# Stacked queries and keys of a differential attention: placed by DMA through DRAM scratch in place of matmuls with a selection matrix

## The chip, the cores and the metric

The kernel is one program on one NeuronCore of a Trainium2 chip (trn2). The metric is the device time of one execution in microseconds (us), taken as the median of several runs. A profile of one execution gives the start, the end and the inferred releaser of every instruction on the five engines: PE (TensorE, matmuls; PEld is its weight load), DVE (VectorE), ACT (ScalarE), POOL (GpSimd) and SP (SyncE, which here does nothing but issue DMAs).

## The reference, cut to what matters

The network has two layers of width 1024 on 512 latent tokens and 256 context tokens. In each layer one input projection feeds three groups of heads: neighbourhood attention, differential attention and gated linear attention. Only the differential attention is touched. It has four heads, each with two components of 32 features, and subtracts a second softmax from a first one:

```python
def diff_weights(q, k, lam):
    s = jnp.einsum('bhcqd,bhckd->bhcqk', q, k).astype(F32) * (q.shape[-1] ** -0.5)
    p = jax.nn.softmax(s, axis=-1)
    return p[:, :, 0] - lam * p[:, :, 1]
...
    qb = rope_2d(rms_norm(_diff_heads(pl['qb']), lp['qn_b']), row, col)
    kb = rope_2d(rms_norm(_diff_heads(pl['kb']), lp['kn_b']), row, col)
    vb = _heads(pl['vb'], DA_HEADS, DA_V_DIM)
...
    o_b = diff_attention_latent(qb, jnp.concatenate([kb, kb_c], axis=3),
                                jnp.concatenate([vb, vb_c], axis=2), lam)
```

In the first layer the context tokens have queries too (768 query tokens), in the second only the latent ones (512). There are always 768 keys.

## The kernel before

A float32 value goes through the matmuls as two parts, a rounded high part and the low rest, so that a product of two values is the sum of high x high, high x low and low x high. A projection is therefore three matmuls for each block of rows (`gemm_steps`, L251 to L253). For the scores of one component of 32 features the kernel packs the four terms into one matmul with 128 rows: the queries stand as high, low, high, low and the keys as high, low, low, high, 32 rows each. These 128-row operands are called stacks. One preparation (`da_prep`, two heads, letter `d` in the order for the first pair and `D` for the second) makes four components of queries and four of keys; it runs four times, twice in each layer.

In the kernel before a stack is filled by TensorE: for a component and a stretch of 512 or 256 tokens, two matmuls with a 32-row selection matrix `stk` copy the high and low parts `hl` onto the right 32-row blocks of a PSUM tile (L770), and DVE (L772) or ACT (L774) casts that tile into the stack tile `st`.

The mixer of a layer is a weave. TensorE's order is written out by hand as a string, `ORDER`: a count advances the stream of projections by so many steps (three matmuls of 512 columns or six of 256), a letter advances one of the threads by one `yield`. Letters of a thread that has ended do nothing. The threads are `d`/`D` (this preparation), `a`, `b` (scores and softmax of the two differential heads, L800), `n`, `l`, `r` (preparation and two heads of the neighbourhood attention), `g` to `q` (gated linear attention). The projections (`pj` for queries and keys, `pjv` for values) go to DRAM through a single tile `x`, from where the threads fetch them again as `xi`, `xv`, `vt`. Every 12 steps a block of the modulation's weights (`ar`, L274, L276) is multiplied in between.

The order on the other engines and on SP is set by a scheduler from its own estimates. All DMAs stand in SP's one queue, in that order, and SP waits at each for what it needs. Projection weights arrive as `wr` (L239) and are split into `wh` and `wl`; `wr` and `ar` share two buffers. The stack tiles `st` share seven buffers with tiles of the other threads; `hl` shares three buffers under the name `P`.

Of the kernel before, what the change touches and what calls it, by code (L numbers as in the profile page):

```python
# [10 lines left out]
F32 = mybir.dt.float32  # L11
F32R = mybir.dt.float32r
# [19 lines left out]
# row blocks of the output projection: those of the heads that are done first, and the last ones  # L32
OUT_A, OUT_B = (0, 1, 2, 3, 4, 5), (6, 7)
# dot products of the modulation's columns: along with a pair of blocks of the MLP, along with a block of its second product
CUTS = 2
ADA_F, ADA_D = 4, 2
# the order of the projections
JOBS = ("gates vb ka0 va0 qb1 kb1 kc0 vc0 qc0 qa1 ka1 va1 kc1 vc1 qc1 gc0 gc1 gc2 gc3",
        "qb0 kb0 vb qa0 ka0 va0 qb1 kb1 qa1 ka1 va1 gates kc0 vc0 qc0 gc0 gc1 kc1 vc1 qc1 gc2 gc3")
# the order of the first steps: norm, modulation by columns (scale, shift), rows of the products  # L40
# [13 lines left out]
# blocks of 32 columns whose windows of four say which copies a part of a stack goes to: (queries, keys) x (high, low)  # L54
WINDOWS = (1, 0, 1, 0, 1, 1, 0, 0, 1)
STACK = ((5, 3), (0, 1))

# columns of the packed per-layer vectors
# [7 lines left out]
# column blocks of w_in (128 columns each)  # L66
# [4 lines left out]
class Lay:  # L71
    """Per-layer vectors on chip."""


class Rows:
    """Row blocks of a product's weights on two tiles of four."""
# [7 lines left out]
class Net:  # L84
# [53 lines left out]
    def setup(self, up):  # L138
        """Constants, and the first layer's vectors."""
# [14 lines left out]
    def tokens(self, p, up):  # L154
        """Two row blocks of the tokens."""
        x = up.tile([128, 2, TT], F32, name=f"x{p}")
        self.nc.sync.dma_start(out=x[:, :, :TL], in_=self.A["xT"][:, 2 * p:2 * p + 2])
        self.nc.sync.dma_start(out=x[:, :, TL:], in_=self.A["ctxT"][:, 2 * p:2 * p + 2])
        self.xs[2 * p], self.xs[2 * p + 1] = x[:, 0], x[:, 1]

    def silu_cond(self, up):
        """Twice silu of both conditioning vectors; the selector halves."""
# [6 lines left out]
    def late_consts(self, up):  # L169
# [5 lines left out]
        sk = up.tile([128, 288], F32, name="sk")  # L175
        self.nc.sync.dma_start(out=sk, in_=self.A["stk"])
        self.stk = self.cp.tile([128, 288], F32R, name="stk")
        self.V.tensor_copy(self.stk, sk)
# [12 lines left out]
    def layer_consts(self, y, up):  # L191
# [17 lines left out]
        # halved convolution weights (column 3 * f + j) and biases  # L209
# [4 lines left out]
    def newton(self, src, n, d):  # L214
        """rsqrt(src / d + EPS) of a compact [128, n]."""
# [8 lines left out]
        # a step of third order (to 8 / 3 of the root), and one of second order  # L224
# [21 lines left out]
    def gemm_steps(self, ps, w, ah, al):  # L246
        """A product; yields after every few steps of it."""
# [18 lines left out]
    def ada_part(self, y, part, pool, bufs):  # L266
        """A sixth of the modulation, 256 columns on each column tile; yields after every block of rows."""
# [22 lines left out]
    def ada_cols(self, fp, parts):  # L290
        """Sixths of the modulation [(layer, part)], columns on the partitions, by dot products of half columns; yields after each."""
# [24 lines left out]
    def ada_chunk(self, y, part, j, up):  # L316
        """256 columns of a sixth of the modulation: the blocks of rows on four column tiles."""
# [20 lines left out]
    def begin(self, y, up):  # L338
        """The first three products run on the scaled tokens; their outputs take the norm, and the shift's own product."""
# [137 lines left out]
    def seg(self, g):  # L477
        """Stream, first token, operands of a segment."""
        s, t0 = (0, g * TC) if g < 2 else (1, 0)
        sl = slice(t0, t0 + TC)  # L480
        hi, lo = ((self.axh, self.axl), (self.ach, self.acl))[s]
        return s, sl, [t[:, sl] for t in hi], [t[:, sl] for t in lo]

    def norm_bcast(self, accs):
        """PSUM [128, 256]: the reciprocal root mean square of each token on every partition."""
# [12 lines left out]
    def make_xn(self, y, xs, g, which, bc=None):  # L498
        """xs(k): the stream's tile and one for its norm (the same without bc: the tile is normed already)."""
# [30 lines left out]
    def pj(self, y, at, name, block, lat=True, ctx=True, perm=False, scale=1.0):  # L530
        """A block's product, on its way to DRAM, from where the head groups fetch it."""
# [17 lines left out]
    def cuts(self, y, name):  # L549
        """A weight that takes the place of two is made ready in parts."""  # L550
# [4 lines left out]
    def pjg(self, y, at, hd, ctxo):  # L555
        """A head's gate: twice its silu."""
# [14 lines left out]
    def pjv(self, y, at, name, block):  # L571
        """Values of 256 columns, tokens on the partitions."""
# [21 lines left out]
    def gates(self, y):  # L594
        """Low-rank gate activations: the weights' two parts side by side (the next product adds their sums)."""
# [35 lines left out]
    def finish(self, y, at, ctxo):  # L631
        """The heads' outputs as operands of the output projection."""
# [19 lines left out]
    def fetch(self, y, ea, hp, hd, cd):  # L652
        """The residual stream takes the place of the tiles that the heads needed first."""
# [10 lines left out]
    def out_first(self, y, ctxo):  # L664
        """The output projection of the heads that are done first."""
# [7 lines left out]
    def head_rms(self, at, xs, G, d, by=None):  # L673
        """Per (tile, token tile, group): reciprocal root mean squares (of the tile times by), compact. Yields ahead of the product."""
# [40 lines left out]
    def to_tokens(self, out, x, n):  # L715
        """x [128 features, n * 128 tokens] to out [128 tokens, n, 128 features]."""
# [15 lines left out]
    def da_prep(self, y, at, d, pr, ctxq):  # L732
# [8 lines left out]
        # the queries' norms go into the exponentials' scales  # L741
        qn = at.tile([128, TT], F32, tag="xn", name="xn", bufs=self.nxn)[:, :Tq]
        S.activation(qn, xq[:, :Tq], AF.Copy, scale=y.g[:, 1:2])
        for i, Tn in ((0, Tq), (1, TT)):
# [14 lines left out]
            # per component of 32 rows: high | low | high | low against high | low | low | high  # L759
            ss = []  # L760
            for c in range(4):
                rows = slice(32 * c, 32 * c + 32)
                if c % 2 == 0:
                    s = at.tile([128, 2, TT], F32R, tag="st", name="st", bufs=self.nst)
                for t0, n in ((0, TL), (TL, TC))[:1 if Tn == TL else 2]:
                    yield
                    ps = self.pm(n)
                    for a in range(2):
                        w = STACK[i][a] * 32
                        T.matmul(ps, lhsT=self.stk[rows, w:w + 128], rhs=hl[rows, a, t0:t0 + n], start=(a == 0), stop=(a == 1))  # L770
                    if (c + i) % 2:
                        V.tensor_copy(s[:, c % 2, t0:t0 + n], ps)  # L772
                    else:
                        S.copy(s[:, c % 2, t0:t0 + n], ps)  # L774
# [7 lines left out]
        # reciprocals of the first softmaxes' sums  # L782
        d.rs = at.tile([128, 6, 2], F32, tag="rs", name="rs", bufs=2)

    def da_head(self, y, at, d, hh, ctxq):
        V, S, T = self.V, self.S, self.T
        for qt in range((TT if ctxq else TL) // 128):
# [18 lines left out]
            # times the first sum, whose reciprocal the outputs' norms take  # L806
# [13 lines left out]
    def values(self, d, qt, vs, ws):  # L820
        """Both heads' weights times values."""
# [7 lines left out]
    def da_out(self, y, at, d, pr, ctxq):  # L829
        """Norms of the outputs, and of the first softmaxes."""  # L830
# [34 lines left out]
    def na_head(self, y, at, d, pr, hh, ctxq):  # L865
# [3 lines left out]
        for qt in range(Tq // 128):  # L869
# [6 lines left out]
            # the scores' columns: segments (first, count, first key), and those with a bias  # L876
# [49 lines left out]
    def gla_prep(self, y, at, d, pr, ctxo):  # L926
        """Gates: 16 * log decay, then its running sums within chunks of 128, forward and backward."""
# [28 lines left out]
        # decays over whole chunks  # L956
# [5 lines left out]
    def gla_states(self, y, at, d):  # L962
        """States at the chunks' starts, both directions (context chunks are 4 and 5)."""
# [475 lines left out]
```

## Time and profile before

| | us |
|---|---|
| median of 3 runs | 1958.68 |
| lowest and highest run | 1957.72, 1968.63 |
| span of the profiled execution (first to last instruction) | 1956.1 |
| median minus that span | 2.6 |
| PE busy | 1874.8 (96% of the span) |
| DVE busy | 1234.8 (63%) |
| ACT busy | 774.1 (40%) |
| DMA | 217.93 MB, 33.8% of the 16 engines' span |

The runs are a list without a note which of them was profiled, so the profiled execution's own time is read as its span with the 2.6 us that lie between it and the median. Two runs lie within 1 us of each other and the third 10 us above. Busy shares are averages over stages; what a change in one stage is worth is read in that stage, from what its engines wait for.

### The profile page before, as it was taken

To read this page: it belongs to the slowest core of one execution; us is meant where nothing else is said; L and a number is where in the kernel's file an instruction comes from. 1 tells how busy PE (TensorE), PEld (TensorE's weight loads), DVE (VectorE), ACT (ScalarE), POOL (GpSimd) and SP (SyncE) were. 2 spreads that over 40 slices of the span, in tenths; PEclk is the share of its full clock that TensorE was granted. 3 is DMA by queue.
4 is the path that set the end of the run, shared out by engine and by line. 5 is a ranking of instruction groups with operands and counts; after the bars stand their busy time and mean duration, and the time that the engine had idled before them with its cause. 6 is when DMAs were issued, how large, how long until landed. Compare 5 with 4: busy or idle time off the path is not lost. (4 is left out here: it accounts for less than half of the span.)

```text
span 1956.1 us, 33522 instructions
## 1 busy us (share of the span) xinstructions
PE 1874.8 (96%) x13598; PEld 1567.2 (80%) x13598; DVE 1234.8 (63%) x2554; ACT 774.1 (40%) x1350; POOL 107.1 (5%) x134
## 2 busy tenths in 40 slices
PE   8999999896999999999999999999996999999999
PEld 6778878774788888888888987878885788888887
DVE  6437575767669786588577563656576675445353
ACT  4536565455234331232133343645545343223232
POOL 2100000101020000000000110000012020000000
PEclk9989999897999999999999999999998989999999
DMA  9423242326122444234434223222433223332322
GB/s 323 138 92 111 92 146 98 115 98 204 54 74 92 124 129 149 94 125 130 139 109 127 95 68 130 84 81 68 143 106 101 65 72 97 97 97 86 109 94 100
DMA packets 90874, 217.93 MB, mean 111 GB/s; under 512 B 10464, under 2 KB 21472, under 8 KB 90592
## 3 DMA queue, kind: packets, MB, share of 16 engines
q1 hardware_dynamic: 90720, 215.79, 33.8%
q8 instruction: 107, 1.75, 0.4%
q14 instruction: 47, 0.39, 0.1%
HBM read 190.06 MB, written 25.69 MB: 110 GB/s over the span
## 5 line engine op out<-in xcount | busy, mean ns | idle before, releaser
L262 ACT CAST wh<-wr 128x1024 fp32r<-128x1024 f32 (+3 forms) x205 | 200.0, 978 | 415.9 <-PE pg L252 222.2
L263 DVE TENSOR_TENSOR wl<-wr,wh 128x1024 fp32r<-128x1024 f32 (+3 forms) x205 | 232.3, 1137 | 168.4 <-ACT wh L262 166.3
L252 PE MATMUL pz<-axl,wh 128*128 128x512 f32 (+1 forms) x752 | 288.3, 383 | 2.6 <-DVE axl L511 2.5
L251 PE MATMUL pz<-axh,wh 128*128 128x512 f32 (+1 forms) x752 | 287.8, 383 | 0.8 <-ACT axh L510 0.7
L253 PE MATMUL pz<-axh,wl 128*128 128x512 f32 (+1 forms) x752 | 287.0, 382 | 0.0
L252 PEld LDWEIGHTS pz<-axl,wh 128*128 128x128 f32 x752 | 142.3, 189 | 29.6 <-DVE axl L511 4.5
L251 PEld LDWEIGHTS pz<-axh,wh 128*128 128x128 f32 x752 | 142.3, 189 | 27.6 <-ACT axh L510 1.8
L253 PEld LDWEIGHTS pz<-axh,wl 128*128 128x128 f32 x752 | 142.3, 189 | 26.9
L308 DVE SCALAR_TENSOR_TENSOR wj<-wc,cb 128x512 bf16<-128x512 f32 x224 | 154.4, 689 | 6.2 <-DMA wc<-in_w_ada_t_dram 1.0
L251 PE MATMUL pg<-axh,wh 128*128 128x512 f32 x344 | 152.9, 445 | 2.7 <-ACT axh L262 2.5
L252 PE MATMUL pg<-axl,wh 128*128 128x512 f32 x344 | 139.3, 405 | 1.8 <-DVE axl L263 1.8
L253 PE MATMUL pg<-axh,wl 128*128 128x512 f32 x344 | 139.0, 404 | 0.0
L251 PE MATMUL pg<-gh,wh 128*128 128x512 f32 (+1 forms) x352 | 133.3, 380 | 0.0
L253 PE MATMUL pg<-gh,wl 128*128 128x512 f32 (+1 forms) x352 | 132.6, 377 | 0.0
L252 PE MATMUL pg<-gl,wh 128*128 128x512 f32 (+1 forms) x352 | 132.0, 375 | 0.0
L1161 DVE SCALAR_TENSOR_TENSOR h<-pg,ada,h 128x512 f32<-128x512 f32 (+1 forms) x80 | 53.5, 669 | 95.0 <-PE pg L253 94.8
L252 PE MATMUL pm<-acl,wh 128*128 128x256 f32 x352 | 99.8, 283 | 0.0
L253 PE MATMUL pm<-ach,wl 128*128 128x256 f32 x352 | 99.6, 283 | 0.0
L251 PE MATMUL pm<-ach,wh 128*128 128x256 f32 x352 | 99.5, 283 | 0.0
L801 DVE TENSOR_REDUCE sm<-pz 128x1 f32<-128x768 f32 (+1 forms) x80 | 67.4, 847 | 45.2 <-PE pz L800 44.5
L251 PEld LDWEIGHTS pg<-axh,wh 128*128 128x128 f32 x344 | 67.2, 195 | 30.8 <-issue 15.7
L1240 ACT ACTIVATE th<-cv 128x512 f32<-128x512 f32 x66 | 37.0, 561 | 121.2 <-DVE cv L1237 121.2
(387 smaller groups left out, 4194.9 us busy)
## 6 DMA issues: line engine op xcount, KB each, us to landing
wc<-in_w_ada_t_dram SPq DMA_DIRECT2D x112, 256.0 KB, 2.9
wr<-in_w_in_dram SPq DMA_DIRECT2D x45, 512.0 KB, 3.8
wr<-in_w_g_dram SPq DMA_DIRECT2D x44, 512.0 KB, 3.5
wr<-in_w_u_dram SPq DMA_DIRECT2D x44, 512.0 KB, 3.4
wr<-in_w_d_dram SPq DMA_DIRECT2D x31, 448.0 KB, 3.2
ar<-in_w_ada_dram SPq DMA_DIRECT2D x48, 256.0 KB, 3.3
ar<-in_w_ada_dram SPq DMA_DIRECT2D x16, 512.0 KB, 7.5
wr<-in_w_d_dram SPq DMA_DIRECT2D x16, 512.0 KB, 3.5
```

The lines of the kernel that those rows point to most:

```text
L251: self.T.matmul(ps, lhsT=wh[:, k, :], rhs=ah[k], start=(k == 0), stop=False)
L252: self.T.matmul(ps, lhsT=wh[:, k, :], rhs=al[k], start=False, stop=False)
L253: self.T.matmul(ps, lhsT=wl[:, k, :], rhs=ah[k], start=False, stop=(k == n - 1))
L262: self.S.copy(hi, x)
L263: (eng or self.V).tensor_tensor(out=lo, in0=x, in1=hi.bitcast(F32), op=ALU.subtract)
L308: V.scalar_tensor_tensor(out=junk, in0=w, scalar=0.5, in1=cb[:, i, h * 512:h * 512 + 512], op0=ALU.mult, op1=ALU.mult, accum_out=acc[:, k, ...
L801: V.tensor_reduce(out=sm[:, c:c + 1], in_=s, op=ALU.max, axis=AX.X, negate=True)
L1161: self.late = V.scalar_tensor_tensor(out=h, in0=ps, scalar=y.ada[part][:, o, s:s + 1], in1=h, op0=ALU.mult, op1=ALU.add).ins
L1240: S.activation(th, c, AF.Tanh)
```

## The change

The selection matrix, its matmuls and the casts of the stacks go. The high and low parts `hl` are written to a DRAM tile `parts` (high, low, and for the keys high once more), and each half of 64 rows of a stack is read back by one DMA whose source is two consecutive parts of 32 rows each: high and low for the queries' halves and the keys' first half, low and high for the keys' second half. The `yield`s between the old matmuls go with them.

```diff
             hl = at.tile([128, 2, TT], F32R, tag="P", name="hl", bufs=3)
             self.split(xn, hl[:, 0, :Tn], hl[:, 1, :Tn])
-            # per component of 32 rows: high | low | high | low against high | low | low | high
+
+            parts = self.dp.tile([2 + i, 128, TT], F32, name=f"hl{y.l}_{pr}_{i}")
+            nc.sync.dma_start(out=parts.rearrange("a p t -> p a t")[:, :2, :Tn], in_=hl[:, :, :Tn].bitcast(F32))
+            if i:
+                nc.sync.dma_start(out=parts[2, :, :Tn], in_=hl[:, 0, :Tn].bitcast(F32))
             ss = []
             for c in range(4):
-                rows = slice(32 * c, 32 * c + 32)
                 if c % 2 == 0:
                     s = at.tile([128, 2, TT], F32R, tag="st", name="st", bufs=self.nst)
-                for t0, n in ((0, TL), (TL, TC))[:1 if Tn == TL else 2]:
-                    yield
-                    ps = self.pm(n)
-                    for a in range(2):
-                        w = STACK[i][a] * 32
-                        T.matmul(ps, lhsT=self.stk[rows, w:w + 128], rhs=hl[rows, a, t0:t0 + n], start=(a == 0), stop=(a == 1))
-                    if (c + i) % 2:
-                        V.tensor_copy(s[:, c % 2, t0:t0 + n], ps)
-                    else:
-                        S.copy(s[:, c % 2, t0:t0 + n], ps)
+                own = parts[:, 32 * c:32 * c + 32, :Tn]
+                for half, src in ((0, own[:2]), (64, own[i:i + 2])):
+                    nc.sync.dma_start(out=s[half:half + 64, c % 2, :Tn].bitcast(F32), in_=src)
                 ss.append(s[:, c % 2])
             stacks.append(ss)
```

The rest of the diff removes `WINDOWS`, `STACK`, the load of `stk` (one DMA and one cast at the start) and comments. Line numbers of the changed kernel differ: L770 has no successor, the writes are L754 and L756, the reads L763, the scores L789.

What the change does to the order is seen at three places. The first is SP's queue in the first layer, first preparation. `ka` and `va` are projections on their way out, `xi` the keys of the neighbourhood attention on their way back. Before:

```order
L239 DMA wr<-in_w_in_dram 128x1024
L547 DMA ka_0_1112<-x 128x768
L274 DMA ar<-in_w_ada_dram 128x512 x2
L239 DMA wr<-in_w_in_dram 128x1024
L845 DMA xi<-ka_0_1112 128x768
```

Now, from the same weight load on:

```order
L754 DMA hl_0_0_1039<-hl 128x2x768
L232 DMA wr<-in_w_in_dram 128x1024
L864 DMA bias<-in_bias_dram 128x256
L763 DMA st<-hl_0_0_1039 64x1x768 x8
L754 DMA hl_0_1_1125<-hl 128x2x768
L756 DMA hl_0_1_1125<-hl 128x768
L540 DMA ka_0_1155<-x 128x768
L763 DMA st<-hl_0_1_1125 64x1x768 x8
L540 DMA va_0_1225<-x 128x768
L834 DMA xi<-ka_0_1155 128x768
```

The way of the neighbourhood attention's keys, out and back, now stands behind 16 reads of stacks and three writes of their parts.

The second is TensorE at the same place. `k_ident,ny` is the broadcast of the keys' norms, `k_rot` the rotation of the keys. Before, behind the sixth matmul of a projection's step:

```order
L770 MATMUL pm<-hl,stk 128x512 x2
L251 MATMUL pg<-ach_87,wh 128x256
L252 MATMUL pg<-acl_95,wh 128x256
L253 MATMUL pg<-ach_87,wl 128x256
L251 MATMUL pg<-ach_88,wh 128x256
L252 MATMUL pg<-acl_96,wh 128x256
L253 MATMUL pg<-ach_88,wl 128x256
L770 MATMUL pm<-hl,stk 128x256 x2
```

Now:

```order
L699 MATMUL pz<-k_ident,ny 32x128 x24
L244 MATMUL pg<-ach_87,wh 128x256
L245 MATMUL pg<-acl_95,wh 128x256
L246 MATMUL pg<-ach_87,wl 128x256
L244 MATMUL pg<-ach_88,wh 128x256
L245 MATMUL pg<-acl_96,wh 128x256
L246 MATMUL pg<-ach_88,wl 128x256
L745 MATMUL pz<-xn,k_rot 128x512
```

The letters that used to step through the queries' stacks now step through the keys' norms and rotation, eight steps (four in the second layer) earlier than before and one projection step apart; the later letters do nothing.

The third is SP's queue in the second layer, first preparation. Before:

```order
L547 DMA ka_1_12405<-x 128x768
L239 DMA wr<-in_w_in_dram 128x1024
L845 DMA xi<-ka_1_12405 128x768
```

Now:

```order
L763 DMA st<-hl_0_0_12183 64x1x512 x8
L754 DMA hl_0_1_12260<-hl 128x2x768
L756 DMA hl_0_1_12260<-hl 128x768
L540 DMA ka_1_12325<-x 128x768
L232 DMA wr<-in_w_in_dram 128x1024
L763 DMA st<-hl_0_1_12260 64x1x768 x8
L540 DMA va_1_12405<-x 128x768
L832 DMA xi<-qa_1_12238 128x512
L834 DMA xi<-ka_1_12325 128x768
```

Here too the tiles that the neighbourhood attention waits for are fetched behind both groups of eight.

## Rows read from the trace of the kernel before

**Rows 1.** The page's head: span, and busy time of each engine.
```profile
span 1956.1 us, 33522 instructions
...
PE 1874.8 (96%) x13598; PEld 1567.2 (80%) x13598; DVE 1234.8 (63%) x2554; ACT 774.1 (40%) x1350; POOL 107.1 (5%) x134
```

**Rows 2.** Windows: length, busy us of engines, PE clock, DMA share, GB/s.
```profile
60.00:560.00 500.00, 470.07 (x4508) 375.74 (x4509) 304.58 (x686) 238.25 (x463) 25.26 (x35) 0.94 0.35 117
119.00:137.00 18.00, 18.00 (x84) 11.47 (x82) 6.53 (x18) 1.90 (x4) 0.00 (x0) 0.59 0.31 103
```

**Rows 3.** Instructions of L770 and casts behind it: duration ns min/median/max, first and last start.
```profile
L770 PE MATMUL pm<-hl,stk x112: 271/387/791, 98.5 to 1319.8; 32*128 32x512 f32 x64, 32*128 32x256 f32 x48
...
L772 DVE CAST st<-pm x28: 416/682/692, 102.1 to 1317.3; 128x512 fp32r<-128x512 f32 x16, 128x256 fp32r<-128x256 f32 x12
```

**Rows 4.** PE in order of time around two pairs of L770: start, us, line.
```profile
103.67 0.39 PE L252 MATMUL pg<-axl,wh 128*128 128x512 f32 x1
103.90 0.40 PE L253 MATMUL pg<-axh,wl 128*128 128x512 f32 x1
104.23 0.72 PE L770 MATMUL pm<-hl,stk 32*128 32x512 f32 x2
104.88 0.50 PE L251 MATMUL pg<-axh,wh 128*128 128x512 f32 x1
...
105.45 0.39 PE L253 MATMUL pg<-axh,wl 128*128 128x512 f32 x1
105.77 0.50 PE L770 MATMUL pm<-hl,stk 32*128 32x256 f32 x2
106.20 0.50 PE L251 MATMUL pg<-axh,wh 128*128 128x512 f32 x1
```

**Rows 5.** DMA issues: count, KB each, median us to landing.
```profile
wr<-in_w_in_dram SPq DMA_DIRECT2D x45, 512.0 KB, 3.8
...
kb<-x SPq DMA_DIRECT2D x3, 384.0 KB, 2.3
```

**Rows 6.** Windows, a stretch in which loads come close together.
```profile
71.00:77.00 6.00, 5.96 (x49) 5.96 (x50) 0.00 (x0) 1.40 (x3) 0.00 (x0) 1.00 0.83 294
```

**Rows 7.** SP in order of time, first layer.
```profile
97.16 0.33 SPq L239 DMA_DIRECT2D wr<-in_w_in_dram  x1
103.83 0.33 SPq L547 DMA_DIRECT2D ka<-x  x1
...
112.97 0.33 SPq L845 DMA_DIRECT2D xi<-ka  x1
```

**Rows 8.** DVE, ACT and PE in order of time, first layer, first preparation.
```profile
95.04 0.95 DVE L263 TENSOR_TENSOR hl<-xn,hl 128x768 fp32r<-128x768 f32 x1
...
111.93 1.01 DVE L712 SCALAR_TENSOR_TENSOR xn<-xi,k_vec,pz 128x768 f32<-128x768 f32 x1 [1.94 <-PE pz L706]
...
116.09 0.85 ACT L679 ACTIVATE xn<-xi 128x768 f32<-128x768 f32 x1 [1.28 <-DMA xi<-ka]
...
119.09 2.73 PE L688 MATMUL pm<-k_ind,xn 128*128 128x2 f32 x24
...
142.41 0.86 PE L800 MATMUL pz<-st 128*128 128x512 f32 x4
```

**Rows 9.** SP and PE, first layer, second preparation.
```profile
220.46 1.24 SPq L875 DMA_DIRECT2D bias<-in_bias_dram  x1
...
235.99 0.64 PE L276 MATMUL pg<-ar,csil 128*32 128x256 f32 x8
...
255.36 0.62 PE L800 MATMUL pz<-st 128*128 128x512 f32 x2
```

**Rows 10.** SP and PE, second layer, first preparation.
```profile
1202.00 0.33 SPq L239 DMA_DIRECT2D wr<-in_w_in_dram  x1
...
1230.11 2.29 PE L688 MATMUL pm<-k_ind,xn 128*128 128x2 f32 x20
```

**Rows 11.** DVE and PE, second layer, second preparation.
```profile
1283.63 0.68 DVE L263 TENSOR_TENSOR hl<-xn,hl 128x512 fp32r<-128x512 f32 x1
...
1320.86 0.87 PE L800 MATMUL pz<-st 128*128 128x512 f32 x4
```

More of the change, by code (lines that the diff above doesn't have):

```diff
@@ L53 @@
      "ooooooooooooooooo"))
-WINDOWS = (1, 0, 1, 0, 1, 1, 0, 0, 1)
-STACK = ((5, 3), (0, 1))
 C_N1, C_N2, C_BADA = 0, 8, 16
@@ L71 @@
 class Lay:
+    pass
 class Rows:
@@ L174, in late_consts @@
         self.nc.sync.dma_start(out=am, in_=self.A["amask"])
[L175 to L178, printed above, removed]
         self.amask = self.cp.tile([128, 5, 32], U8, name="amask")
@@ L1415, in pack @@
     A["rot"] = rot
-    A["stk"] = np.concatenate([(p[:, None] % 32 == np.arange(32)[None]) * f4(w) for w in WINDOWS], axis=1)
     am = np.zeros((128, 5, 32), f4)
```

## The prediction

> **What bounds the kernel now.** I read the page's head first, for the engine that could set the time: PE is busy for 1874.8 of 1956.1 us [rows 1]. The windows then say whether that holds where the change lies: from 60 to 560 us PE is busy for 470 of 500 us at a granted clock of 0.94, while DMA is busy to 35% [rows 2]. So here, too, a matmul that goes is time that goes, up to the point where something else is waited for. DMA has spare capacity on the mean, but that is a mean over 16 engines, and a wait is set by when one transfer lands. Third come the groups of L770 and of the casts behind it, for how often and how long [rows 3], and PE in order of time around two of them, for the pitch from one instruction's start to the next, since durations of pipelined matmuls overlap [rows 4]. Last I read SP, DVE and PE in order of time in the four preparations, to lay the new transfers on that time line [rows 7 to 11]. The reader should look there for the instant at which `hl` is complete, for when PE first needs something behind it, and for what stands between them on SP's queue.
>
> **What goes.** The 112 matmuls are 56 pairs, 32 on 512 columns and 24 on 256 [rows 3]. Around a wide pair, L253 starts at 103.90 and L251 behind the pair at 104.88, 0.98 us; from L252 to L253 without a pair are 0.23. The pair costs 0.75. Around a narrow one it is 106.20 − 105.45 − 0.23 = 0.52 [rows 4]. That is 32 × 0.75 + 24 × 0.52 = 36.5 us, all on PE and none beside other PE work. The casts, 0.68 us at the median, 28 on DVE [rows 3] and as many on ACT, lie beside a busy PE on engines that are busy to 63% and 40% [rows 1]: I give them 0. If PE had waited for them, the gain would be larger by a few us.
>
> **What moves.** The keys' norm broadcast and rotation come eight letters earlier, one projection step apart. Between them DVE multiplies by the norm (L712), 1.01 us [rows 8]; a step of three matmuls at 0.23 covers 0.7. I take 0.5 us of waiting in each of four preparations, 2 us; the bounds are 0 and 1 each.
>
> **What comes.** Twelve writes of `hl` and 64 reads of 64 rows: 48 of 64 × 3072 bytes = 196,608 and, for the second layer's queries, 16 of 131,072. Some 19 MB, small against 218. Issuing costs SP 0.33 us each [rows 7], 21 us spread over four places on an engine that only issues. A write should land as `kb` does, 2.3 us after issue for the same 384 KB [rows 5].
>
> What a read takes is not in this trace. The nearest row for the pace is the stretch where loads come closest: 294 GB/s at 83% of 16 engines [rows 6], so 294 / (16 × 0.83) = 22.1 GB/s for one busy engine. A read spread over 16 engines is then 0.56 us of moving, with a landing near the 2.3 to 3.8 us of [rows 5]; on two engines 4.4 us, on one 8.9. The loads and projection round trips of [rows 5, 7] have 128 rows outermost on both sides. The new reads have 64 on one side and 2 × 32 on the other, since high and low lie a whole part apart. I take a transfer to be cut along its outermost count, on both sides alike, so that it can be shared out two ways here and not 16: 4.4 us a read and 35.5 us for a group of eight (8 × 131,072 bytes: 23.7). This is a choice by the shape, not shown by a row; the bounds are 0.56 and 8.9. Further, I take it that every such read goes to the same two engines, and that a wide transfer issued behind a group has its share on those two queued behind it.
>
> The Trainium skill, DMA: Bandwidth & Descriptors, section "Why a DMA increments its semaphore by 16 and not by 1", has this as a rule: the number of engines is the largest up to 16 that divides the outermost count (above one) of both sides, and they are the lowest-numbered ones. By it the reads have two engines, the same two each time. No row of before has such a shape, so the trace neither agrees nor disagrees. Its section "Queues, rings and completion order" adds that one engine takes descriptors up in the order of the ring, which is the queueing behind a group.
>
> Laid on the time line, less what PE has gained since the place began:
>
> *First layer, first preparation.* The last part of `hl` starts at 95.04 and takes 0.95 [rows 8]; a weight load stands at 97.16 on SP [rows 7]. The write lands about 99.6, the eight queries' reads at 135.1. The keys' writes add 5 us (2.3 with the bytes of the third part and the queue), and their reads end at 140.1 + 35.5 = 175.6. Behind all this stands `xi<-ka`, which came at 112.97 before [rows 7]. Its square on ACT is 0.85 (L679), and PE's 24 matmuls on it (L688) started at 119.09 [rows 8]. They would be reached at 114.0, eight pairs being gone by then (4 × 0.75 + 4 × 0.52 = 5.1). They start at about 177: 63 us of waiting.
>
> *First layer, second preparation.* The groups stand behind `bias` at 220.46 [rows 9], which comes 3.8 earlier (six pairs). A first block of four queries' and four keys' reads from about 217 ends at 253, and a load of `ar` that PE needs at L276 lies behind it. L276 started at 235.99 [rows 9], now 230.2 (5 × 0.75 + 4 × 0.52 earlier): 24 us.
>
> *Second layer, first preparation.* From the load at 1202.00 [rows 10], 1.5 earlier: 1200.9 + 23.7 + 5 + 35.5 + 1.5 for two squares = 1266.5. L688 is at 1230.11 [rows 10], less 8 × 0.75 + 4 × 0.52 = 8.1: 1222. That is 44 us.
>
> *Second layer, second preparation.* `hl` is complete at 1284.31 [rows 11]; 3 us for the write, then 23.7 + 5 + 35.5, is 1351.5. The scores behind it started at 1320.86 [rows 11], now 1312.8: 39 us.
>
> The waits are 63 + 24 + 44 + 39 = 170 us, in place of 36.5 saved. The profiled execution is 1956.1, and the median lies 2.6 above that span. 1956.1 − 36.5 + 2 + 170 + 2.6 = **2094 us**.
>
> The clock is left at 0. In 119 to 137 us it is granted at 0.59 with PE busy throughout, near the half level (1.2 of 2.4 GHz), right behind 24 matmuls of two columns and a wait [rows 2, 8]. A new wait might bring such a stretch: 18 us at half speed lose some 9, four times 36 at most. That goes into the range, as does the fact that a stretch like it stands there already.
>
> **Rivals.** *The reads are spread over 16 engines* (the other side, faster). The mechanism is the same queue with the price of [rows 6] in place of mine: from `hl` to complete stacks a write of 3.6 to 5, eight issues of 0.33 and a landing of 4, some 12 us. The keys' part of `xi<-ka` would come only a few us later than at 112.97, so 0 to 6 us of waiting in all: 1956.1 − 36.5 + 2 + 3 + 2.6 = 1927 (1924 to 1930 with that wait, and a little around it for the moved letters). For it: nothing in the trace shows a transfer held to few engines. Against it: nothing there has this shape.
>
> *Narrow reads that hold up nobody else.* If the wide transfers behind a group pass it by, only the stacks' own readers wait. In the first preparation the first scores are at 142.41 [rows 8], less all 16 pairs of the preparation (8 × 0.75 + 8 × 0.52 = 10.2 us) 132.2, against 171.6 for the last stack (without the queueing in the 5 us): 39 us. In the second they are at 255.36 [rows 9], now 245, against 253: 8. In the second layer some 38 and 34. Together 119: 2043 us. For it: a queue's transfers share 16 engines, 14 of them free. Against it: a 128-row load has rows for all 16, and is not complete before the last.
>
> *The change does not do what it says*, or saves on PE what was never waited for: the written order shows the matmuls gone and the reads there, and PE is 96% busy [rows 1], so this has next to nothing.
>
> Between the two sides: for a group of eight that takes G us, the four sums above give waits of 2 G − 8, G − 11.5, 1.67 G − 15 and 1.67 G − 20. They come to the 34 us (36.5 − 2) that the change saves at G = 14, thus at five engines (8 × 8.9 / 5). Above that the change gains, below it loses.
>
> **How the numbers follow.** Forecast 0.62, narrow reads that hold up nobody else 0.2, spread reads 0.13, something between that ends near zero 0.05. Within 1% is about what a measurement of this kernel cannot tell from no change. The first two are slower by 4 to 7%: slower 0.82, same 0.05, faster 0.13. The range reaches from under the second case, with an engine pace a third better than 22.1 GB/s, 2000, to the forecast with the clock's 36 us and some 25 more of queueing, 2155. Left out are the spread case, the middle, and reads on a single engine.
>
> **What would show it.** In the changed profile the reads L763 should end their group 35 us after its first issue if narrow and in order (24 for the second layer's queries), and under 8 if spread. In the windows, DMA's mean share during a group should be near 2/16, with few GB/s, while SP stands waiting. PE's idle time should lie before L688, L276 and the scores, put down to a DMA of `xi`, `ar` or `st`, with about 63, 24, 44 and 39 us. The steps of the projections should keep a pitch of 0.23 without pairs between them, and a wait for L712 of no more than 1 us should stand before the rotation. I am wrong if the groups land fast, since everything but the 36.5 and the 2 hangs on that; and too high if the weights and `xi` overtake the reads. I am too low if weight loads, which share the queue, stop the projections besides.

## The result, and the profile after

The changed kernel takes 2124.49 us (median of 4 runs, 2123.26 to 2127.12) against 1958.2 (median of 4 runs, 1951.24 to 1968.63), a ratio of 1.0861 (95% interval 1.0817 to 1.0905). The forecast was 2094 us with a range of 2000 to 2155. Of all the runs in this document one stands apart, 9292 us in e4 beside three of 2113 to 2115, and e4's ratio is taken without it.

The head of the page of the changed kernel, to be laid beside [rows 1]:

```profile
span 2121.5 us, 33387 instructions
...
PE 1870.5 (88%) x13486; PEld 1564.9 (74%) x13486; DVE 1223.4 (58%) x2525; ACT 761.2 (36%) x1322; POOL 106.6 (5%) x134
```

PE stands idle for 2121.5 − 1870.5 = 251 us, before for 1956.1 − 1874.8 = 81.3: 169.7 us of new waiting. Its busy time fell by only 4.3 us, though 112 matmuls are gone. The first is what the prediction summed to 172; the second is where it was off.

Windows of the changed kernel (columns as in [rows 2]): the same stretch as there, and one of 16 us inside the first group of keys' reads.

```profile
140.00:156.00 16.00, 2.80 (x16) 2.44 (x14) 0.00 (x0) 0.00 (x0) 0.00 (x0) 0.61 0.13 49
60.00:560.00 500.00, 380.42 (x3574) 306.25 (x3575) 250.60 (x580) 209.95 (x415) 23.94 (x34) 0.87 0.36 125
```

A share of 0.13 of 16 engines is 2.1 engines, at 49 GB/s together. A group of 8 × 196,608 bytes takes 32 us at that pace, where the prediction had 35.5. Over the long stretch the share is 0.36, as before: the mean hides it.

SP in order of time, first layer, first preparation (start, duration, line, tile):

```profile
99.54 18.68 SPq L763 DMA_DIRECT2D st<-hl  x8
118.33 0.39 SPq L754 DMA_DIRECT2D hl<-hl  x1
118.76 6.07 SPq L756 DMA_DIRECT2D hl<-hl  x1
124.88 0.94 SPq L540 DMA_DIRECT2D ka<-x  x1
135.80 19.47 SPq L763 DMA_DIRECT2D st<-hl  x8
155.37 3.68 SPq L540 DMA_DIRECT2D va<-x  x1
159.09 0.82 SPq L834 DMA_DIRECT2D xi<-ka  x1
```

SP itself is stopped within a group: eight issues take 18.68 us, where eight of 0.33 would take 2.6. `ka`, which went out at 103.83 before [rows 7], leaves at 124.88, and `xi<-ka` starts at 159.09, before at 112.97.

What that does to PE, in order of time (in brackets the idle time before the row and its releaser):

```profile
138.39 0.80 PE L244 MATMUL pg<-axh,wh 128*128 128x512 f32 x1 [26.31 <-ACT x L537]
138.98 0.63 PE L245 MATMUL pg<-axl,wh 128*128 128x512 f32 x1
139.41 0.63 PE L246 MATMUL pg<-axh,wl 128*128 128x512 f32 x1
139.83 0.63 PE L244 MATMUL pg<-axh,wh 128*128 128x512 f32 x1
...
174.76 2.72 PE L681 MATMUL pm<-k_ind,xn 128*128 128x2 f32 x12 [31.95 <-ACT xn L672]
...
311.36 1.07 PE L269 MATMUL pg<-ar,csil 128*32 128x256 f32 x4 [26.59 <-DMA ar<-in_w_ada_dram]
...
1323.35 0.98 PE L789 MATMUL pz<-st 128*128 128x512 f32 x2 [23.23 <-DMA st<-hl]
...
1350.24 4.42 PE L681 MATMUL pm<-k_ind,xn 128*128 128x2 f32 x20 [10.13 <-ACT xn L672]
...
1439.89 1.97 PE L815 MATMUL pm<-wn,vn 128*64 128x128 f32 x14 [14.35 <-ACT wn L715]
```

Most rows name an engine as the releaser that only passes a DMA's lateness on. ACT's `x` (L537) is the single tile on a projection's way out, which is not free until `ka<-x` has read it; ACT's `xn` (L672) is the square of the `xi` that comes back behind the groups; before L815, ACT's `wn` (L715) hangs on a load of `bias`, for which DVE (L891) waits 14.8 us. ACT in order of time says when the first two transfers had landed:

```profile
137.74 0.87 ACT L537 ACTIVATE x<-pg 128x512 f32<-128x512 f32 x2 [32.83 <-DMA ka<-x]
173.86 0.84 ACT L672 ACTIVATE xn<-xi 128x768 f32<-128x768 f32 x1 [35.25 <-DMA xi<-ka]
```

That is 12.9 us after the issue of `ka<-x` and 14.8 us after that of `xi<-ka`, which in the kernel before took 3.0. So a transfer behind a group is late twice: SP issues it late, and it lands late. The three PE rows from 138.98 on also show the lower clock: 0.43 us from one start to the next, where [rows 4] have 0.23.

### The profile page after: what moved, and what is told of

It is laid out like the page before. It is cut to its first block, busy times and chain, and to the rows that moved or that the text cites. A ratio compares the mean times of both kernels' runs of the same rounds, so it can differ in the third digit from the quotient of the medians.

```text
span 2121.5 us, 33387 instructions
## 1 busy us (share of the span) xinstructions
PE 1870.5 (88%) x13486; PEld 1564.9 (74%) x13486; DVE 1223.4 (58%) x2525; ACT 761.2 (36%) x1322; POOL 106.6 (5%) x134
## 5 line engine op out<-in xcount | busy, mean ns | idle before, releaser
L244 PE MATMUL pz<-axh,wh 128*128 128x512 f32 (+1 forms) x752 | 291.3, 387 | 0.7 <-ACT axh L503 0.7
L244 PE MATMUL pg<-axh,wh 128*128 128x512 f32 x344 | 153.2, 445 | 30.5 <-ACT x L537 29.4
L244 PEld LDWEIGHTS pz<-axh,wh 128*128 128x128 f32 x752 | 142.3, 189 | 30.4 <-ACT axh L503 1.5
L244 PE MATMUL pg<-gh,wh 128*128 128x512 f32 (+1 forms) x352 | 132.5, 377 | 0.1
L244 PEld LDWEIGHTS pg<-axh,wh 128*128 128x128 f32 x344 | 68.6, 199 | 55.4 <-ACT x L537 29.8
L244 PE MATMUL pm<-ach,wh 128*128 128x256 f32 x352 | 99.3, 282 | 0.0
L794 ACT ACTIVATE P<-pz,sm,ny 128x768 f32<-128x768 f32 (+1 forms) x80 | 72.6, 909 | 50.8 <-DVE sm L793 32.5
```

The lines of the kernel that those rows point to most:

```text
L244: self.T.matmul(ps, lhsT=wh[:, k, :], rhs=ah[k], start=(k == 0), stop=False)
L794: S.activation(P[:, c, :nk], s, AF.Exp, bias=sm[:, c:c + 1], scale=rq, accum_out=sm[:, 2 + c:3 + c])
```

## The experiments

Median, ratio to the kernel before and PE's idle time (span minus busy time, of the profiled execution; 81.3 before, 251 in the changed kernel). The kernel before was run again beside each set of experiments, with medians from 1952.67 to 1959.03 us, so differences between experiments are taken from the ratios:

| run | us | ratio (95% interval) | span | PE busy | PE idle |
|---|---|---|---|---|---|
| e1 reads of 32 rows | 1990.0 | 1.0176 (1.0153 to 1.0198) | 1983.8 | 1857.9 | 125.9 |
| e2 packed scratch | 1982.84 | 1.0139 (1.0120 to 1.0159) | 1982.2 | 1852.5 | 129.7 |
| e3 four blocks | 2060.11 | 1.0534 (1.0516 to 1.0553) | 2055.7 | 1864.0 | 191.7 |
| e4 narrow, steps back | 2114.4 | 1.0813 (1.0786 to 1.0840) | 2111.1 | 1870.8 | 240.3 |
| e5 reads on POOL | 1972.48 | 1.0072 (1.0043 to 1.0101) | 1969.6 | 1849.9 | 119.7 |
| e6 packed, steps back | 1966.22 | 1.0034 (1.0021 to 1.0047) | 1960.4 | 1847.1 | 113.3 |
| e7 matmuls doubled | 1983.49 | 1.0117 (1.0093 to 1.0140) | 1981.0 | 1899.5 | 81.5 |
| e8 tile to tile | 1965.91 | 1.0045 (1.0020 to 1.0070) | 1968.7 | 1859.4 | 109.3 |
| e9 no matmuls | 1914.69 | 0.9806 (0.9784 to 0.9827) | 1913.0 | 1832.4 | 80.6 |
| e10 POOL, steps back | 1977.4 | 1.0127 (1.0102 to 1.0153) | 1979.4 | 1852.6 | 126.8 |
| e11 tile to tile on POOL | 1942.92 | 0.9949 (0.9933 to 0.9966) | 1942.9 | 1850.2 | 92.7 |
| e12 e11 and a spare tile | 1931.07 | 0.9875 (0.9843 to 0.9907) | 1925.2 | 1834.0 | 91.2 |

**How many engines: e1, e2, e3.** The theory was that two blocks outermost confine a read to two engines; the first rival, that the round trip and the number of transfers on SP's queue cost the time; the second, the moved letters. In e1 each read is cut in two:

```diff
-                for half, src in ((0, own[:2]), (64, own[i:i + 2])):
-                    nc.sync.dma_start(out=s[half:half + 64, c % 2, :Tn].bitcast(F32), in_=src)
+                for b in range(4):
+                    nc.sync.dma_start(out=s[32 * b:32 * b + 32, c % 2, :Tn].bitcast(F32), in_=own[b % 2 + i * (b // 2)])
```

> The changed kernel with each read of 64 rows made as two reads of 32, so that both sides have 32 rows outermost: twice the transfers (128), the same bytes, the same order of the threads. Theory (a read whose source has two blocks outermost is moved by two engines, and what stands behind it waits): a group of sixteen reads takes some 6 to 8 us in place of 32 (98,304 bytes over 16 engines at 24.5 GB/s are 0.25 us, an issue 0.35 us), the waits of PE in the four preparations fall from some 165 us to under 10, the share of time at the lower clock goes back with them, and the time is 1920 to 1935 us, faster than the kernel before by 1.2 to 2%. Rival 1 (the round trip through scratch and the number of transfers on SP's one queue cost the time, not the engines): with twice the transfers the waits stay or grow, 2100 us or more. Rival 2 (the moved letters cost it): no change, about 2124 us.

In e2 the reads stay 64, and the scratch is laid out anew:

```diff
+            parts = self.dp.tile([4, 2 + i, 32, TT], F32, name=f"hl{y.l}_{pr}_{i}")
...
+                own = hl[32 * c:32 * c + 32, :, :Tn].bitcast(F32)
+                nc.sync.dma_start(out=parts[c].rearrange("a p t -> p a t")[:, :2, :Tn], in_=own)
+                if i:
+                    nc.sync.dma_start(out=parts[c, 2, :, :Tn], in_=own[:, 0])
...
+                own = parts[c].rearrange("a p t -> (a p) t")[:, :Tn]
+                for half, r in ((0, 0), (64, 32 * i)):
+                    nc.sync.dma_start(out=s[half:half + 64, c % 2, :Tn].bitcast(F32), in_=own[r:r + 64])
```

> The changed kernel with another layout of the scratch: per component of 32 rows, the parts one behind the other, so that a read of 64 rows finds its source in one block. As many reads (64) of the same size, and the writes split by component (48 in place of 12). Theory (two engines): both sides of a read have 64 rows outermost, it is spread, a group of eight takes 5 to 7 us, and the time is 1920 to 1935 us. Rival 1 (round trip and number of transfers): 112 transfers in place of 76, the writes in front of the reads, the time no better than 2124 us. Rival 2 (moved letters): about 2124 us.

In e3 each 32 rows are two blocks of 16 with a gap:

```diff
-            parts = self.dp.tile([4, 2 + i, 32, TT], F32, name=f"hl{y.l}_{pr}_{i}")
+            parts = self.dp.tile([4, 2 + i, 2, 17, TT], F32, name=f"hl{y.l}_{pr}_{i}")
...
-                own = parts[c].rearrange("a p t -> (a p) t")[:, :Tn]
+                own = parts[c].rearrange("a b p t -> (a b) p t")[:, :16, :Tn]
-                for half, r in ((0, 0), (64, 32 * i)):
-                    nc.sync.dma_start(out=s[half:half + 64, c % 2, :Tn].bitcast(F32), in_=own[r:r + 64])
+                for half, r in ((0, 0), (64, 2 * i)):
+                    nc.sync.dma_start(out=s[half:half + 64, c % 2, :Tn].bitcast(F32), in_=own[r:r + 4])
```

> As the packed layout, but each part of 32 rows is kept as two blocks of 16 rows with a spare row behind each, so that the source of a read of 64 rows has four blocks outermost that cannot be joined. The writes go by 16 rows (24 a preparation's pair of tensors). Theory: four engines, a group of eight takes 16 to 17 us in place of 32; by the sums of the prediction the waits are 2 x 16 - 8, 16 - 11.5, 1.67 x 16 - 15 and 1.67 x 16 - 20, together 47 us, the clock costs some 9 (in proportion of the 32 us that it cost with 165 us of waits), and the time is 1956.1 - 36.5 + 2 + 47 + 9 + 2.6 = 1980 us (1960 to 2010). If the number of engines had nothing to do with it, it would be as the changed kernel or worse for its additional writes, 2124 us or more; if a source of several blocks were slow as such, whatever their number, also 2124.

Windows of e2 in the first preparation, of e3 inside a group:

```profile
106.00:122.00 16.00, 6.73 (x46) 5.32 (x44) 1.03 (x2) 0.00 (x0) 0.00 (x0) 0.77 0.99 258
```

```profile
126.00:130.00 4.00, 0.00 (x0) 0.00 (x0) 0.00 (x0) 0.00 (x0) 0.00 (x0) 0.50 0.25 91
```

Two blocks: a share of 0.13. Four: 0.25, four engines. 64 rows in one block: 0.99, with writes and weights moving in the same window; a read lands 2.5 to 5.6 us after its issue, and eight are issued within 8 us, in place of 32 us for a group. So on SP's queue the shape sets the number of engines, and e1 and e2 take 135 and 142 us off while they issue more transfers than the changed kernel. Rival 1 falls as the main cause.

But all three times are well over what the theory gave. e2 shows why: the engines are full for 16 us at 258 GB/s. The first preparation moves 0.8 and 1.2 MB out and 3.1 MB back, 5 MB, which is 20 us at that pace, and the weights want the same engines. The waits of PE in e2 (us in total, times, longest):

```profile
PE pg L244 <- ACT x L537: 20.7, 3, 10.4
PE pm L714 <- DVE np L901: 15.2, 3, 13.6
```

The projections still wait for their way out, behind two groups on SP. In e3 the expected 47 us of waits were 191.7 − 81.3 = 110. SP in order of time there shows what the estimate had left out, the keys' writes, which SP issues from 106.41 to 123.67 before the first read of the keys:

```profile
109.80 0.32 SPq L758 DMA_DIRECT2D hl<-hl  x1
111.78 0.31 SPq L760 DMA_DIRECT2D hl<-hl  x1
113.73 0.30 SPq L758 DMA_DIRECT2D hl<-hl  x1
115.71 0.31 SPq L760 DMA_DIRECT2D hl<-hl  x1
```

Here the small writes leave 2 us apart, about the 2.2 us of one read of 196,608 bytes at 91 GB/s, as if each waited for one of the reads ahead to end; no run tests that.

**The moved letters: e4.** The steps of the threads are put back, the reads stay narrow:

```diff
             for c in range(4):
+                for _ in range(1 if Tn == TL else 2):
+                    yield
```

> The changed kernel with its narrow reads, and the threads' steps put back where the matmuls and casts had been: each component's reads are reached as many letters later as before the change, and the keys' norm and rotation come where they did. It undoes the move alone. Theory (two engines): a group still takes 32 us on two engines, and the keys' group starts later (by the eight letters, some 10 us), so the waits stay or grow a little: 2110 to 2150 us. Rival 2 (the moved letters cost it): back to the kernel before less the matmuls, 1925 to 1960 us.

2114.4 us: 10 us less than the changed kernel, of the 166 that it lost, and the intervals of the two ratios overlap. The moved letters are not the cause.

**Which queue, and all at once or not: e5, e6.** In e5 the change is one word, `nc.gpsimd` for `nc.sync` in the line of the reads.

> The changed kernel with the 64 narrow reads issued by POOL on its own queue, the writes left on SP's. It separates the two engines from SP's order: weights, the projections' way out and back no longer stand behind the groups on SP, but share the two engines with them. If the hold-up on SP's queue is most of the cost (theory), the waits before the projections and the norms' matmuls go, those before the scores stay, and the time is that of the prediction's second case plus some clock, 2030 to 2075 us. If order on the queue has no part and only the sharing of two engines counts, it stays at 2110 to 2130 us. If reads issued by POOL are spread over more engines, it comes to 1980 to 1990 us as the spread reads did.

A window of e5 in the first preparation, and the packets, MB and share of the 16 engines of the two queues in it (q1 is SP's, q0 POOL's):

```profile
106.00:120.00 14.00, 9.62 (x64) 7.86 (x62) 1.02 (x2) 0.61 (x2) 1.86 (x5) 1.00 0.99 283
```

```profile
q1 hardware_dynamic: 975, 2.53, 58.0%
q0 software_dynamic: 1387, 1.42, 40.0%
```

The reads on POOL's queue take 40% of the engines' time here, 6.4 engines, and SP's own transfers take the rest. Issued by POOL the narrow reads are not held to two engines, so e5 can't tell order from sharing, which was its purpose. It landed under its third case and 0.67% (13 us) under e2. An SP queue without the reads may be worth that much, but e2 also has 48 writes where e5 has 12. e6 is e2 with the two lines of e4.

> The packed layout (reads spread over 16 engines, 1982.8 us), with the threads' steps put back between the components, so that the reads come two at a time over some 10 to 20 us and not all at once. Theory for what is left of the loss: the groups now fill all 16 engines for some 20 us (5 MB at 245 GB/s) and the projections' way out through the one tile waits behind them on SP; spaced out, most of the 20 us before L244 and of the 15 us before L714 go: 1945 to 1965 us. Rival: what is left has nothing to do with the burst (the added bytes and transfers cost it wherever they stand): 1978 to 1990 us.

1966.2 us is 1 us above what the theory gave, and 1.05% of the time before (some 20 us) below e2. Part of this can be the letters themselves, whose return was worth some 10 us in e4. The share of the engines, 0.99 in e2 from 106 to 122 us, is 0.76 in the same stretch of e6 and in this window of 20 us:

```profile
98.00:118.00 20.00, 16.55 (x141) 13.27 (x139) 4.98 (x7) 3.98 (x7) 1.47 (x3) 0.98 0.76 211
```

**What the matmuls had cost: e7, e9.**

```diff
-                    for a in range(2):
+                    for a in (0, 1, 0, 1):
```

> The kernel before with each stack's two matmuls done twice (the high and the low part are added up twice, so the stacks' values are double). It measures the price of what the change removes. Theory (the pairs lie on PE's path at the pitch that the rows showed, 0.75 and 0.52 us): 36.5 us more than the kernel before, 1988 to 1996 us. Rival (PE would have waited there anyway, so that their removal could give nothing): within 10 us of the kernel before.

```diff
-                    ps = self.pm(n)
-                    for a in range(2):
-                        w = STACK[i][a] * 32
-                        T.matmul(ps, lhsT=self.stk[rows, w:w + 128], rhs=hl[rows, a, t0:t0 + n], start=(a == 0), stop=(a == 1))
+                    ps = xn[:, t0:t0 + n]
```

> The kernel before with the 112 matmuls of the stacks left out; the casts stay and read the rotated input in place of the matmuls' tile, so that the stacks hold other values. It measures what the removal gives when nothing comes in its place. By the prediction's pitches 36.5 us, 1918 to 1924 us. The doubled pairs cost 25 us, since the second pair of the same shape pays the streaming alone: if that is the whole price, 1930 to 1936 us. If PE would have to wait for the casts' engines, less still.

In e7 `start` is set at each high part, so the second pair begins the sum afresh and the stacks keep their values; they are not doubled. e7 adds 24.7 us of busy PE, under the theory: the second pair of a shape pays its columns alone, 32 × 0.46 + 24 × 0.23 = 20 us, and 5 besides. e9 gives 1.94% of the kernel before, 38 us, and PE's idle time stays at 80.6. So 36.5 was right (the interval is 34 to 42 us), and the whole of it was to be had.

**Straight from tile to tile: e8, e11, and both together: e10.**

```diff
+                own = hl[32 * c:32 * c + 32, :, :Tn]
+                for b in range(4):
+                    nc.sync.dma_start(out=s[32 * b:32 * b + 32, c % 2, :Tn].bitcast(F32), in_=own[:, (b + i * (b // 2)) % 2].bitcast(F32))
```

This stands in place of scratch, writes and reads, with the steps of e4; in e11 it is `nc.gpsimd`.

> No scratch: each block of 32 rows of a stack is moved by one DMA from the tile of the high and low parts straight to its place, 128 transfers with 32 rows outermost on both sides, the threads' steps as before the change. 12.5 MB of moving in place of 12.5 read and 6 to 7 written, no writing out first. If what is left of the loss with spread reads is bytes on the engines and the round trip: 1925 to 1955 us. If it is the number of transfers on SP's queue (128, 42 us of issuing): 1975 us or more.

> The changed kernel with its 64 reads issued by POOL (where they are spread over all engines, as e5 showed) and the threads' steps put back, so that the stacks come two transfers at a time. e5 took 14 us off the spread reads on SP by leaving SP's queue free, e6 took 17 off by spacing them. If the two are separate causes, 1945 to 1958 us, even with the kernel before or under it. If both remove the same wait (the projections' way out behind a group on SP), no better than either: 1963 to 1973 us.

> Each block of 32 rows straight from the tile of the high and low parts to its place, 128 transfers issued by POOL, steps put back, no scratch. SP's queue has no additional transfer at all, and the bytes are two thirds. If bytes and the round trip through scratch are what is left of the loss: 1935 to 1955 us. If POOL's issuing (0.65 us each, some 83 us, in front of its own multiplications for the rotation) is in the way: 1965 us or more.

e8 moves 11.5 MB, since the second layer's queries are shorter, not 12.5. It lies between its two cases and settles nothing alone; with the same 128 transfers on POOL, e11 is another 0.96% (19 us) faster, so issuing them from POOL is worth that much, and e11 passes the kernel before by 0.51% (0.34 to 0.67%). e10 falls under neither of its cases, it is slower than e5. In POOL's order of time the reads of a group still go eight in one piece, and the keys' group goes at 130.94 (in e5 at 122.87):

```profile
100.34 5.41 POOL L765 DMA_DIRECT2D st<-hl  x8 [18.75 <-DMA hl<-hl]
106.92 1.29 POOL L747 TENSOR_TENSOR t<-xn,k_cosT 128x512 f32<-128x512 f32 x1 [1.17 <-DVE xn L705]
...
130.94 5.29 POOL L765 DMA_DIRECT2D st<-hl  x8 [22.55 <-DMA hl<-hl]
```

There the steps only made the keys later; the scores then waited 36.5 us for stacks, in e5 18.5, in e11 9.3 us, as the waits of PE say for e10 and for e11:

```profile
PE pz L791 <- DMA st<-hl: 36.5, 7, 14.6
```

```profile
PE pz L787 <- DMA st<-hl: 9.3, 4, 3.2
```

**The place of the weights: e12.** PE is busy 17.8 us longer in e11 than in e9. The groups of the MLP's matmuls, which no edit touches, show a part of it (busy us, mean ns). Before, in the changed kernel, and in e12:

```profile
L252 PE MATMUL pz<-axl,wh 128*128 128x512 f32 (+1 forms) x752 | 288.3, 383 | 2.6 <-DVE axl L511 2.5
```

```profile
L245 PE MATMUL pz<-axl,wh 128*128 128x512 f32 (+1 forms) x752 | 291.6, 388 | 2.6 <-DVE axl L504 2.4
```

```profile
L247 PE MATMUL pz<-axl,wh 128*128 128x512 f32 (+1 forms) x752 | 289.1, 384 | 2.6 <-DVE axl L506 2.5
```

Over the three groups of such matmuls (the others are `axh,wh` and `axh,wl`) that is 863.1 us before, 873.8 in the changed kernel, 876.0 in e11 and 865.3 in e12. These are sums of durations that overlap. What counts is the pitch from one start to the next: its mean is 227.3 ns before and in e9, 232.9 in the changed kernel, 232.8 in e11 and 227.4 in e12, and 5.5 ns over 2256 matmuls are 12 us. With the selection matrix, 1152 bytes of each partition went, and the tiles behind it, the weights' among them, moved down by as much. e12 is e11 with

```diff
+        pad = self.cp.tile([128, 288], F32, name="pad")
+        self.V.memset(pad[:, :1], 0.0)
```

> The best version so far (e11: straight from tile to tile, issued by POOL, steps put back; 1942.9 us), with an unused tile of 1152 bytes a partition in the place in which the selection matrix stood, so that the weight tiles lie at the addresses of the kernel before. All kernels without the matrix have a pitch of some 233 ns between the matmuls of the MLP, which the change does not touch, and the three that have it 227 ns, over some 2250 matmuls 12 to 13 us. Theory (where the weight tiles lie sets that pitch): 227 ns again, and 1929 to 1934 us, 1.1 to 1.3% faster than the kernel before. Rival (the pitch comes from something else that went with the matrix, the stacks' way of being filled or the order): 233 ns, and 1940 to 1946 us.

The 12 us are back, and e12 is 1.25% (0.93 to 1.57%) faster than the kernel before. That the place of the tiles behind the matrix sets the pitch is shown. Of what these matmuls read, only the weight tiles lie there (`axh` and `axl` lie ahead of it), which speaks for the weights; but other tiles moved along, and why this place and not that one stays open.

## Why the prediction held, step by step

**Two engines in order, right.** The share of 0.13 and the 32 us a group (35.5 in the prediction) are as forecast, and so is the queueing behind a group: `xi<-ka`, issued at 159.09, landed by 173.86, and PE came to L681 at 174.76, forecast was 177. How much of this is SP's stop in issuing, which the sum had at 0.33 us an issue, and how much the two engines' queue, no run separates. The Trainium skill, DMA: Bandwidth & Descriptors, section "Why a DMA increments its semaphore by 16 and not by 1", has the engines as the largest number up to 16 that divides both outermost counts: here the trace agrees, with 2.1 engines for two blocks, 4 for four and, with other transfers beside them, all for 64 rows. For POOL's queue the same section has transfers of fewer engines start at ones that move on from transfer to transfer; the 6.4 engines of e5's reads fit that, but do not tell it from reads that are each spread.

**The waits, right in sum, only in part in their places.** The first preparation of the first layer: 26.3 + 32.0 = 58 (forecast 63), in two places where one was named: the projections stop first, at their way out. The prediction had a stop of the projections only in its last sentence, and put it to weight loads. The second: 26.6 at L269 and 5 before scores, 32 (24). The second layer: 23.2 + 5.6 + 3.5 + 10.1 = 42 (44), of which only the 10.1 lie before L681, where the forecast had all, and the rest before scores; then 14.4 + 9.2 + 6.4 = 30 (39), a part of it not before scores but before the neighbourhood attention's values and the gates of the linear attention. The rotation's wait for L705, 2 us in the sum, was 1.3.

**What goes, right.** 36.5 us against 38 in e9.

**The clock, mis-sized.** It stood at 0 with a bound of 36. PE should be busy for 1874.8 − 36.5 = 1838.3 us and is for 1870.5, 32 more. Of that 12 is the MLP's pitch, which no step foresaw. The other 20 are put to the clock: behind the wait of 26.3 us the projections run at 0.43 us in place of 0.23. Busy time times the share of the clock that was not granted, summed over stretches of 2 us, is 42 us in the kernel before and 62 in the changed one, which agrees; no run takes the clock alone. The mean clock over the span, 0.974 before and 0.934 now, counts idle stretches too: from 112 to 138.4 us it is 0.55, and PE is busy for 0.09 us. The stretch by which the prediction set its bound, 119 to 137 us of the kernel before, has no wait of PE in front of it. With both, 1956.1 − 36.5 + 169.7 + 12 + 20 = 2121, the span. That the range held in spite of the 12 us is luck: it kept that room for the clock and for queueing.

**The rivals.** Narrow reads that hold up nobody else (2043) is excluded by PE's rows at L244, L681 and L269, which wait for transfers behind the groups, and by their landing after 12.9 and 14.8 us. The spread case was wrong as priced: it gave 1927 with a group of 12 us hidden, and by the break-even anything above five engines gains. Spread reads on SP (e1, e2) lose 1.4 to 1.8%. The prediction priced one group by itself, 12 us. In e2 the writes, both groups and the weights want the engines at once, which are full for 16 us; `ka<-x` stands behind both groups and is issued at 117.63 in place of 103.83; and the 12 us of pitch come on top.

## What to carry to other kernels

A DMA's price is set by its shape before its size: read the outermost counts of both sides, since on SP's queue few blocks outermost meant few engines (issued by POOL they did not), and on an in-order queue everything behind them is late as well. A share of DMA time that is a mean over 16 engines hides this; look at the window in which the group moves, and at who stands behind it on the queue. When a burst is spread, add its bytes to what the engines have to bring in that window anyway, and if a constant goes, look whether the tiles behind it have moved.

## What the runs showed of the hardware that was not expected

- The same matmuls of the MLP had a mean pitch of 232.9 ns in place of 227.3 when the weight tiles, with all else behind the matrix, lay 1152 bytes lower, and of 227.4 with a spare tile in the gap.
- Narrow reads issued by POOL took 40% of the 16 DMA engines' time beside SP's transfers (all together 0.99, 283 GB/s); the same reads issued by SP, alone, took 0.13 at 49 GB/s.
- One preparation's writes and spread reads, with the weights beside them, filled the engines to 0.99 for 16 us at 258 GB/s.
- Transfers of 128 rows issued behind a group of narrow reads landed after 12.9 and 14.8 us, one of them after 3.0 in the kernel before.
